# Weight sums of the down projection on GpSimd: made during the up projection instead of during the heads

## The chip, the cores and the metric

The kernel runs on one core of one Trainium2 chip, in one launch. Time is device time in microseconds (us), as the median of several runs. Engines have their short names: PE (TensorE matmul), PEld (TensorE weight load), DVE (VectorE), ACT (ScalarE), POOL (GpSimd), SP (SyncE, whose queue here issues nearly all transfers).

## The reference

One layer of a hybrid decoder for a prompt of 1024 tokens and 8 single tokens (1032 columns): a norm, an input projection, eight HGRN2 heads beside a Mamba-2 mixer, an output projection with residual, and then a gated MLP. The change concerns the MLP's last weight, `w_down`:

```python
h = rmsnorm(x, w['norm2_w'])
gate, val = jnp.split(h @ w['w_up'], 2, axis=-1)
gate, buf_f_new = causal_dwconv(gate, buf_f, w['ffn_conv_w'], w['ffn_conv_b'])
x = x + (jax.nn.silu(gate) * val) @ w['w_down']     # (1032, 2816) @ (2816, 1024)
```

## The kernel before

All matrix products run in fp32 precision as three products of rounded parts (high x high, high x low, low x high). The program is written as one stream of matmuls in a fixed order on PE (`manual_schedule`); the other engines' instructions are placed by a scheduler, in an order that is fixed when the program is built, and each engine works through its own in that order. Work that goes beside the matmuls is handed out by a count of matmul steps: `after(n, work)` (a list that `tick` counts down) and `spread(pieces, n)`, which takes the next piece of a generator every n ticks, one tick for each matmul of the main stream.

The stages on the profile's clock: input projection and scan of the mixer to some 390 us; the heads (390 to 880, the rest of the input projection runs between their matmuls); the output projection with the second norm (to some 1050); the up projection (to about 1500); the down projection.

The MLP's two products use a fast 2x2 block scheme with seven block products, named `p1` to `p7`. For the down projection four of the seven need sums of weight blocks. `down_sums` (L1192) makes them ahead: 22 pieces, for each of 11 row blocks and 2 column halves. A piece fetches 2 x 256 KB of `w_down` to a tile `wq` (L193, in `fetch`), adds on POOL four times 128x256 in place (L1202), and stores 512 KB to `wsum_d` in device memory (L1204). The tile has tag "g" with one buffer, so a piece's fetch comes behind the store of the piece before. The down projection reads `wsum_d` in `dw_load`, first in its unit 0, which is loaded during the last channel tile of the up projection (`last_step`).

In the kernel before, these pieces start with the job "conv" (L1220), after the second head's projection, one step of a piece every 26 ticks, and run during heads 1 to 6.

The up projection (`ups`, L1649) goes over 22 channel tiles `j`. A tile has 14 products, (name, half) for seven names and two halves of the tokens, each 12 matmuls of 258 columns, so 168 ticks in a tile. From the second tile on they come in the order `p1 p6 p5 p7 p2 p4 p3`, both halves of each. What belongs to one tile:

- `up_load` (L1394): two loads of 512 KB of up weights `ws` for the next tile (L1401), each to one of two buffers, on SP.
- `up_sums` (L1410): four sums `wt` of 128x512 on POOL (L1417), of both loads.
- `up_split` (L1427): the rounded parts `wh` on ACT (L1440) and the rests `wl` on DVE (L1441), two names at a time.
- `Up`: evictions. `p1` and `p5` are copied by ACT (`us`, L1463 and L1471), `p6`, `p7`, `p2`, `p4` and `p3` are added by DVE (L1467, L1475, L1483, L1491, L1498). After `p7` POOL makes `val` (L1476) and `us` (L1477) for that half; DVE's eviction of `p3` (L1498) reads this `us`.
- `up_close`: convolution, SiLU and product on ACT and DVE; `act_sets` stores the activation's blocks to `act_d` (L1521, SP), 4 stores for an even tile, and for an odd one 10, both in the tile after.

Products `p1`, `p7`, `p3` go to three psum banks in turn (`ua`), the other four to four banks (`ub`): so `p4` of a half takes the bank that `p5` of the same half left.

Of the kernel before, what the change touches and what calls it, by code (L numbers as in the profile page):

```python
# [51 lines left out]
def hybrid_layer(  # L52
# [30 lines left out]
    def tl(tag, name, dt=F32):  # L83
        w, n = TAGS[tag]
        return (work if tag in ("hT", "big", "e", "g") else tmp).tile([P, w], dt, tag=tag, bufs=n, name=nm(name))
# [104 lines left out]
    def fetch(dst, src):  # L190

        with tc.issue_after(last_w[0].ins):
            SP.dma_start(dst, src)  # L193
# [44 lines left out]
    def job(name, load, run):  # L238
        jobs.append((name, load, run))

    def after(n, work):

        item = [n, work]
        later.append(item)
        return item
# [7 lines left out]
    def tick():  # L253
        for item in list(later):
            item[0] -= 1
            if item[0] <= 0:
                later.remove(item)
                item[1]()

    def spread(pieces, n, then=None):  # L260

        def go():
            if next(pieces, 0) is None:
                after(n, go)
            elif then is not None:
                then()
        go()
# [75 lines left out]
    def conv_state(src2d, nrow, ntile, out):  # L343
        def rows(j0):
            rt = half("rt")
            nj = min(4, ntile - j0)
            fetch(rt[:nrow, :nj * P], src2d[:, j0 * P:(j0 + nj) * P])
            return rt, nj

        nxt = rows(0)  # L350
        for j0 in range(0, ntile, 4):
            yield
            (rt, nj), nxt = nxt, rows(j0 + 4) if j0 + 4 < ntile else None
            ps = bank("cst", "nx")
            for j in range(nj):
                PE.transpose(ps[:, j * nrow:(j + 1) * nrow], rt[:nrow, j * P:(j + 1) * P], ident[:nrow, :nrow])
            V.tensor_copy(out[:, j0:j0 + nj, :], ps[:, :nj * nrow].rearrange("p (j r) -> p j r", r=nrow))
# [407 lines left out]
    def ssm_conv_state():  # L765
        for j0 in range(0, XT, 4):
            yield
            ps = bank("l11", "nx")
            for j in range(4):
                PE.transpose(ps[:11, j * P:(j + 1) * P], last11[:, j0 + j, :], ident)  # L770
            csr = keep.tile([16, 512], F32, tag="csr", bufs=1, name=nm("csr"))
            V.tensor_copy(csr[:11, :512], ps[:11, :])
            cl = slice(j0 * P, (j0 + 4) * P)
            SP.dma_start(cs_prompt[0, 0, :, cl], csr[0:3, :512])
            SP.dma_start(cs_sample[0, :, 2, cl], csr[3:11, :512])
        SP.dma_start(cs_sample[0, :, 0:2, :], state_conv_ssm[0, :, 1:3, :])
# [16 lines left out]
    def once(work):  # L793
        def run():
            work()
            return
            yield
        return run
# [63 lines left out]
    def head_in(h):  # L862
        t = {}

        def f_end():
            f, k = t["f"], tl("big", "k")
            A.activation(f[:, :NT], f[:, :NT], AF.Identity, bias=lbt[:, 0, h:h + 1], scale=lbt[:, 1, h:h + 1])
            V.tensor_scalar(k[:, :NT], f[:, :NT], -1.0, 1.0, op0=ALU.mult, op1=ALU.add)
            t["k"] = k

        for n, off, func in (("f", OFF_F, AF.Sigmoid), ("q", OFF_Q, AF.Silu), ("v", OFF_I, AF.Copy),
                             ("sg", OFF_G, AF.Silu)):
            def evict(c, cs, ps, n=n, func=func):
                t["out"] = A.activation(t[n][:, cs], ps, func)

            def begin(n=n):
                t[n] = tl("e" if h == 0 and n == "f" else "big", n)

            if h == H - 1 and n == "sg":
                in_job_last(f"{n}{h}", off + h * P, evict, begin)  # L880
            else:
                in_job(f"{n}{h}", off + h * P, evict, begin, f_end if n == "f" else None)
        return t
# [308 lines left out]
    def down_sums():  # L1192
        src = w_down[0].rearrange("(i two p) (gv h c) -> h i p two gv c", two=2, p=P, gv=2, h=2)
        for i in range(DK):
            for h in range(2):
                t = tl("g", "wq")[:, :DM]
                for two in range(2):
                    fetch(t[:, two * 512:(two + 1) * 512].rearrange("p (gv c) -> p gv c", gv=2), src[h, i][:, two])
                yield
                g1, v1, g2, v2 = (t[:, n * 256:(n + 1) * 256] for n in range(4))  # L1200
                for out, x_, y_ in ((v2, v1, v2), (v1, g1, v1), (g1, v2, g1), (g2, g1, g2)):
                    G.tensor_tensor(out, x_, y_, op=ALU.add)  # L1202
                yield
                SP.dma_start(wsum_d[h].rearrange("q m p k c -> p k (q m) c")[:, i],  # L1204
                             t.rearrange("p (q c) -> p q c", c=P))
                yield
# [3 lines left out]
    def conv_states():  # L1210
        yield from ssm_conv_state()
        yield from conv_state(state_conv_ffn[0].rearrange("b r d -> (b r) d"), 16, FT, fbufT)
        yield
# [3 lines left out]
    heads[0] = head_in(0)  # L1217
    ssm_gate(1)
    heads[1] = head_in(1)
    job("conv", None, once(lambda: (spread(conv_states(), 60), spread(down_sums(), 26))))  # L1220
    for h in range(2, H):
        heads[h] = head_in(h)

# [425 lines left out]
    def ups(j, seq):  # L1649

        us_ = up_open(j)
        for n, (name, i) in enumerate(seq):
            yield from us_[i].mul(name)
            if n == 2 and j + 1 < FT:
                up_load(j + 1)
            if n == 5 and j == 0:
                up_sums(1)
            if n in (5, 9, 13) and j + 1 < FT:
                up_split(j + 1, (5, 9, 13).index(n))
            if n == 1 and j:  # L1660
                up_split(j, 3)
            if j == FT - 1:
                last_step(n)
        up_close(j, us_[0])

    with tc.manual_schedule(engines={mybir.EngineType.PE}):
# [25 lines left out]
        after(24, lambda: spread(second, 1))  # L1692
        for _ in ups(0, [(name, i) for i in range(2) for name in FIRST]):
            tick()
        for j in range(1, FT):
            for _ in ups(j, [(name, i) for name in ORDER for i in range(2)]):
                tick()
# [134 lines left out]
```

## Time and profile before

| | us |
|---|---|
| median of three timed runs (lowest, highest) | 1748.21 (1746.71, 1750.33) |
| the profiled execution, its own time | 1748.51 |
| its span, first to last instruction | 1746.6 |
| PE busy | 1704.6 (98%) |
| DVE busy | 1180.5 (68%) |
| ACT busy | 838.3 (48%) |
| POOL busy | 485.6 (28%) |
| POOL adds on `wq`, 88 of them, from 433.9 to 786.7 | 83.3 |

In rows of the profile an instruction has its start, its length, engine, line, operation and its tiles as out<-in; in brackets stands how long its engine was idle before it and what ended that. `x4` is four in a row. In lists of waits three numbers stand behind each pair: us in total, how often, and the longest. The table of stretches gives each engine's busy time and, in brackets, its instructions. Busy time of PE is made of pipelined matmuls, so a busy PE is not PE at its peak.

### The profile page before, as it was taken

The numbers are of one execution on the slowest core, as the hardware profiler recorded it, in microseconds if no ns is written. First come the engines' busy times: TensorE is split into PE (matmuls) and PEld (weight loads), VectorE is DVE, ScalarE is ACT, GpSimd is POOL, SyncE is SP. The second block draws the span as 40 slices with busy tenths as digits, with TensorE's granted clock in tenths as the row PEclk, the third lists the DMA queues.
The fourth block names the chain that finished last, engine by engine and source line by source line (L and its number), as shares of the span: only waits on it lengthen the run. The fifth ranks groups of instructions, "written<-read, shape, count | busy, mean of one in ns | idle before, by whom it ended". The sixth has DMA issues, their size and how long they took to land.

```text
span 1746.6 us, 39082 instructions
## 1 busy us (share of the span) xinstructions
PE 1704.6 (98%) x15967; PEld 1650.3 (94%) x15967; DVE 1180.5 (68%) x2053; ACT 838.3 (48%) x1507; POOL 485.6 (28%) x500
## 2 busy tenths in 40 slices
PE   7999999999999999999999998999999999999998
PEld 7999998998999999999899998999999999999998
DVE  4657888467755655664755678867777777775664
ACT  6478688443443444444344444334433334444344
POOL 1102242111433422440102124554445554000001
PEclk9999999999999999999999999999999999999999
DMA  5133574563444443444556442323333323786463
GB/s 158 37 82 93 144 211 139 154 178 120 147 140 127 133 147 111 139 131 124 159 169 204 127 136 58 104 92 95 101 113 113 92 92 96 251 270 229 152 190 123
DMA packets 319689, 239.31 MB, mean 137 GB/s; under 512 B 18380, under 2 KB 287734, under 8 KB 319494
## 3 DMA queue, kind: packets, MB, share of 16 engines
q1 hardware_dynamic: 319222, 236.72, 45.1%
q8 instruction: 125, 2.05, 0.5%
q14 instruction: 54, 0.44, 0.1%
q0 software_dynamic: 288, 0.10, 0.0%
HBM read 178.18 MB, written 58.77 MB: 136 GB/s over the span
## 4 chain that ended last, share of the span: by engine, by line
PE 41%; DVE 4%; DMA 2%; ACT 1%; issue 1%; SPq 1%; DVEq 0%; ACTq 0%
PE ub L94 13%; PE dn L94 11%; PE ua L94 9%; PE mm L94 7%; DMA at<-act_d 1%; DMA ws<-in_w_out_dram 1%; DVE x L1320 1%; DVE wl L1094 0%; PE fin L1761 0%; SPq L193 0%; DVE ul L1331 0%; DMA x<-x_d 0%; DVE wl L1441 0%; DMA act_d<-fext 0%; DVE fcv L370 0%
## 5 line engine op out<-in xcount | busy, mean ns | idle before, releaser
L94 PE MATMUL mm<-hh,wh 128*128 128x344 f32 x1248 | 406.5, 326 | 0.0
L94 PE MATMUL mm<-hl,wh 128*128 128x344 f32 x1248 | 403.9, 324 | 0.0
L94 PE MATMUL mm<-hh,wl 128*128 128x344 f32 x1248 | 402.9, 323 | 0.0
L94 PEld LDWEIGHTS mm<-hh,wh 128*128 128x128 f32 x1248 | 234.9, 188 | 2.9 <-issue 0.9
L94 PEld LDWEIGHTS mm<-hh,wl 128*128 128x128 f32 x1248 | 235.1, 188 | 2.1 <-issue 1.0
L94 PEld LDWEIGHTS mm<-hl,wh 128*128 128x128 f32 x1248 | 234.9, 188 | 2.2 <-issue 0.9
L94 PE MATMUL ub<-uh,wh 128*128 128x258 f32 x704 | 199.4, 283 | 2.1 <-DVE fext L1491 1.6
L94 PE MATMUL ub<-ul,wh 128*128 128x258 f32 x704 | 199.6, 283 | 1.5 <-DVE ul L1352 1.5
L94 PE MATMUL ub<-uh,wl 128*128 128x258 f32 x704 | 198.8, 282 | 0.0
L94 PE MATMUL mm<-mx,wh 128*128 128x258 f32 x1024 | 190.9, 286 | 3.2 <-DVE mx L1110 2.3
L94 PEld LDWEIGHTS mm<-mx,wh 128*128 128x128 f32 x1024 | 158.5, 189 | 5.2 <-DVE mx L1110 2.7
L94 PE MATMUL dn<-at,wh 128*128 128x260 f32 (+1 forms) x896 | 163.1, 282 | 0.0
L94 PE MATMUL ua<-uh,wh 128*128 128x258 f32 x528 | 149.2, 283 | 1.1 <-ACT us L1463 0.6
L94 PE MATMUL ua<-ul,wh 128*128 128x258 f32 x528 | 148.9, 282 | 0.0
L94 PE MATMUL ua<-uh,wl 128*128 128x258 f32 x528 | 148.4, 281 | 0.0
L94 PE MATMUL mm<-mx,wl 128*128 128x258 f32 x512 | 145.4, 284 | 1.7 <-DVE wl L1094 1.7
L94 PEld LDWEIGHTS dn<-at,wh 128*128 128x128 f32 x896 | 137.6, 188 | 0.0
L1202 POOL TENSOR_TENSOR wq<-wq 128x256 f32<-128x256 f32 x88 | 83.3, 947 | 189.0 <-DMA wq<-in_w_down_dram 149.6
L94 PEld LDWEIGHTS ub<-uh,wh 128*128 128x128 f32 x704 | 132.9, 189 | 2.5 <-ACT uh L1330 1.8
L94 PEld LDWEIGHTS ub<-ul,wh 128*128 128x128 f32 x704 | 133.1, 189 | 1.9 <-DVE ul L1352 1.9
L94 PEld LDWEIGHTS ub<-uh,wl 128*128 128x128 f32 x704 | 133.1, 189 | 0.0
L94 PE MATMUL dn<-at,wl 128*128 128x260 f32 (+1 forms) x448 | 126.6, 283 | 2.8 <-DVE wl L1607 2.8
(341 smaller groups left out, 3711.9 us busy)
## 6 DMA issues: line engine op xcount, KB each, us to landing
ws<-in_w_in_dram SPq DMA_DIRECT2D x52, 512.0 KB
ws<-in_w_up_dram SPq DMA_DIRECT2D x44, 512.0 KB
at<-act_d SPq DMA_DIRECT2D x77, 258.0 KB
ws<-in_w_out_dram SPq DMA_DIRECT2D x36, 512.0 KB
wq<-in_w_down_dram SPq DMA_DIRECT2D x44, 256.0 KB
wsum_d<-wq SPq DMA_DIRECT2D x22, 512.0 KB
mx<-mix_d SPq DMA_DIRECT2D x32, 258.0 KB
csb<-cs_d SPq DMA_DIRECT2D x32, 256.0 KB
```

The source lines that it names most:

```text
L94: PE.matmul(out, lhsT, rhs, start=start, stop=stop)
L1202: G.tensor_tensor(out, x_, y_, op=ALU.add)
L1320: V.scalar_tensor_tensor(x_, x_, col("n2", m), rs, op0=ALU.mult, op1=ALU.mult)
```

## The change

The 22 pieces are handed out in the up projection, from the start of its second channel tile, one step every 19 ticks, and no longer from the job "conv". A piece has seven steps instead of three: after the fetch two empty ones, then the first add, the second, the third with the fourth, the store. At 7 x 19 = 133 ticks a piece this makes five pieces in about four tiles of 168 ticks.

```diff
                 yield
+                yield
+                yield
                 g1, v1, g2, v2 = (t[:, n * 256:(n + 1) * 256] for n in range(4))
                 for out, x_, y_ in ((v2, v1, v2), (v1, g1, v1), (g1, v2, g1), (g2, g1, g2)):
                     G.tensor_tensor(out, x_, y_, op=ALU.add)
-                yield
+                    if x_ is not v2:
+                        yield
                 SP.dma_start(wsum_d[h].rearrange("q m p k c -> p k (q m) c")[:, i],
                              t.rearrange("p (q c) -> p q c", c=P))
                 yield
...
-    job("conv", None, once(lambda: (spread(conv_states(), 60), spread(down_sums(), 26))))
+    job("conv", None, once(lambda: spread(conv_states(), 60)))
...
         for _ in ups(0, [(name, i) for i in range(2) for name in FIRST]):
             tick()
+        spread(down_sums(), 19)
         for j in range(1, FT):
```

The number and kinds of instructions stay as they are; the order on PE, DVE and ACT stays the same to the row, and only POOL's and SP's change. (Lines behind the first edit are 3 or 4 higher in the changed kernel: L1401 is L1404 there, L1417 is L1420, L1202 and L1204 are L1204 and L1207.)

SP of the kernel before, in channel tile 4 of the up projection: the last activation stores of tile 2, the two loads of up weights `ws` for tile 5, and the first stores that follow.

```order
L1521 DMA act_d<-fext_13056 128x256
L1521 DMA act_d<-fext_13056 128x260
L1401 DMA ws_13653<-in_w_up_dram 128x8x128
L1401 DMA ws_13655<-in_w_up_dram 128x8x128
L1521 DMA act_d<-val_13326 128x256
```

SP of the changed kernel at the same place:

```order
L1524 DMA act_d<-fext_12891 128x256
L1524 DMA act_d<-fext_12891 128x260
L193 DMA wq_13276<-in_w_down_dram 128x2x256
L1207 DMA wsum_d<-wq_13276 128x8x128
L193 DMA wq_13499<-in_w_down_dram 128x2x256 x2
L1404 DMA ws_13512<-in_w_up_dram 128x8x128
L1207 DMA wsum_d<-wq_13499 128x8x128
L1404 DMA ws_13514<-in_w_up_dram 128x8x128
L193 DMA wq_13698<-in_w_down_dram 128x2x256
L1524 DMA act_d<-val_13170 128x256
```

The end of piece 4 (`wq_13276`), all of piece 5 (`wq_13499`) and the first fetch of piece 6 stand where the two loads of up weights stood alone, and the store of piece 5 stands between the two. The same picture comes again four, eight and twelve tiles later.

POOL of the kernel before, from the end of tile 3's group of sums to tile 4's group (`wt` of `ws_13653` and `ws_13655`):

```order
L1417 TENSOR_TENSOR wt_13392<-wt_13388,ws_13382 128x512
L1502 MEMSET fext_13588 128x2
L1504 COPY fext_13588<-fbufT 128x8x2
L1476 TENSOR_TENSOR val_13326<-us_13422,us_13458 128x258
L1477 TENSOR_TENSOR us_13380<-us_13422,us_13380 128x258
L1476 TENSOR_TENSOR val_13326<-us_13437,us_13475 128x258
L1477 TENSOR_TENSOR us_13407<-us_13437,us_13407 128x258
L1417 TENSOR_TENSOR wt_13657<-ws_13655 128x512
```

POOL of the changed kernel at the same place:

```order
L1420 TENSOR_TENSOR wt_13239<-wt_13235,ws_13229 128x512
L1505 MEMSET fext_13443 128x2
L1507 COPY fext_13443<-fbufT 128x8x2
L1204 TENSOR_TENSOR wq_13276<-wq_13276 128x256 x3
L1479 TENSOR_TENSOR val_13170<-us_13270,us_13309 128x258
L1480 TENSOR_TENSOR us_13227<-us_13270,us_13227 128x258
L1204 TENSOR_TENSOR wq_13276<-wq_13276 128x256
L1479 TENSOR_TENSOR val_13170<-us_13288,us_13326 128x258
L1480 TENSOR_TENSOR us_13255<-us_13288,us_13255 128x258
L1204 TENSOR_TENSOR wq_13499<-wq_13499 128x256 x4
L1420 TENSOR_TENSOR wt_13516<-ws_13514 128x512
```

Piece 4 is split around the first half's `val` and `us`, three adds ahead of them and one behind; piece 5's four adds stand ahead of the next group of sums.

## The prediction

> **What bounds the kernel now.** The page comes first, for the engine that is busy all the time; then the table of stretches, for the stage that the work leaves and the stage that it enters.
>
> ```profile
> PE 1704.6 (98%) x15967; PEld 1650.3 (94%) x15967; DVE 1180.5 (68%) x2053; ACT 838.3 (48%) x1507; POOL 485.6 (28%) x500
> L1202 POOL TENSOR_TENSOR wq<-wq 128x256 f32<-128x256 f32 x88 | 83.3, 947 | 189.0 <-DMA wq<-in_w_down_dram 149.6
> ...
> core 0: us, PE busy (x) PEld busy (x) DVE busy (x) ACT busy (x) POOL busy (x), PEclk, DMA share, GB/s
> 430.00:800.00 370.00, 365.31 (x4787) 347.65 (x4787) 225.77 (x370) 160.46 (x247) 133.51 (x124) 1.00 0.45 133
> 1080.00:1500.00 420.00, 418.88 (x3490) 418.46 (x3489) 313.64 (x551) 168.09 (x303) 199.43 (x206) 1.00 0.34 106
> 1080.00:1100.00 20.00, 19.37 (x162) 19.16 (x161) 17.43 (x28) 9.56 (x17) 11.17 (x9) 1.00 0.27 81
> ```
>
> TensorE is busy in both stages, the heads (430 to 800) and the up projection (1080 to 1500). What the change can win is what TensorE waits for in the heads; what it can lose is a wait that the up projection hardly has today. So the waits of TensorE and of its weight loads are read next, first for 430 to 800, then (last two rows) for 1080 to 1500.
>
> ```profile
> PE a L94 <- DVE q L925: 2.3, 4, 1.2
> PE a L94 <- issue: 1.7, 1, 1.7
> PE cst L356 <- DVE od L699: 0.5, 1, 0.5
> PEld a L94 <- DVE tt L927: 1.1, 5, 0.2
> PEld cst L356 <- DVE od L699: 0.8, 1, 0.8
> PEld cst L356 <- DVE sg L1054: 0.2, 1, 0.2
> ...
> PE ua L94 <- ACT us L1463: 0.6, 1, 0.6
> PE ua L94 <- DVE val L1498: 0.5, 1, 0.5
> ```
>
> The 88 adds run on POOL, which no wait of TensorE names. They touch TensorE only through VectorE: 2.3 us of waits for `q` (L925) and 0.5 for the reciprocal root (L699); with the weight loads' waits for VectorE (1.1, 0.8, 0.2) that is 4.9 us. In the up projection TensorE waits 1.1 us in 420.
>
> **The change part by part.** *Leaving the heads.* The 83.3 us of adds and the 66 transfers go from a place where nobody waits for them. The gain is at most the 4.9 us above and at least nothing, since some of those waits are for VectorE's own chain. I take 2.3, the four waits for `q`, the row that names a VectorE step which shares its time with the adds.
>
> *Entering the up projection: room on POOL.* 88 adds of 947 ns are 83 us more on POOL's 199.43 of 420: 67%, so POOL does not become the bound on average. What counts is the order on POOL and on SP. One channel tile of the up projection lasts 20.2 us (1240.87 to 1261.03 in the first fence below, two successive weight loads). In it POOL makes four weight sums `wt`, then `val` and `us` for each half, and is free for some 10 us before the next weights land.
>
> ```profile
> 1240.87 4.81 SPq L1401 DMA_DIRECT2D ws<-in_w_up_dram  x2
> 1261.03 4.80 SPq L1401 DMA_DIRECT2D ws<-in_w_up_dram  x2
> ...
> 1249.07 1.46 POOL L1417 TENSOR_TENSOR wt<-ws 128x512 f32<-128x512 f32 x1 [9.63 <-DMA ws<-in_w_up_dram]
> ...
> 1254.79 0.11 POOL L1502 MEMSET fext<- 128x2 f32 x1
> ...
> 1255.42 1.19 POOL L1476 TENSOR_TENSOR val<-us,us 128x258 f32<-128x258 f32 x1
> 1256.58 0.74 POOL L1477 TENSOR_TENSOR us<-us,us 128x258 f32<-128x258 f32 x1
> ...
> 1269.41 1.43 POOL L1417 TENSOR_TENSOR wt<-ws 128x512 f32<-128x512 f32 x1 [10.67 <-DVE fext L1548]
> ```
>
> In the changed order most pieces stand either in that free time or, three adds and one, around the first `val` and `us`. The exception is where two pieces follow each other without a `wt` group between them: pieces 4 and 5, 9 and 10, 14 and 15, 19 and 20, in channel tiles 4, 8, 12 and 16. SP then has: store of the first piece, two fetches of the second, the first half of the next up weights, the store of the second piece, and only then the second half of the up weights. SP is one queue: the fetch reuses the only `wq` buffer and waits for the store to land, the second store waits for POOL, and the up weights `ws` are queued behind it. How long each link takes stands in the heads, where the same transfers run: store to next fetch, fetch to POOL's start, and four adds.
>
> ```profile
> 547.12 0.37 SPq L1204 DMA_DIRECT2D wsum_d<-wq  x1
> ...
> 550.52 1.20 SPq L193 DMA_DIRECT2D wq<-in_w_down_dram  x2
> 555.58 3.82 POOL L1202 TENSOR_TENSOR wq<-wq 128x256 f32<-128x256 f32 x4 [8.49 <-DMA wq<-in_w_down_dram]
> ...
> 603.15 1.20 SPq L193 DMA_DIRECT2D wq<-in_w_down_dram  x2
> 607.40 3.50 POOL L1202 TENSOR_TENSOR wq<-wq 128x256 f32<-128x256 f32 x4 [7.69 <-DMA wq<-in_w_down_dram]
> ...
> 629.01 1.21 SPq L193 DMA_DIRECT2D wq<-in_w_down_dram  x2
> 635.47 3.18 POOL L1202 TENSOR_TENSOR wq<-wq 128x256 f32<-128x256 f32 x4 [11.71 <-DMA wq<-in_w_down_dram]
> 781.55 5.16 POOL L1202 TENSOR_TENSOR wq<-wq 128x256 f32<-128x256 f32 x4
> ```
>
> Put on the tile quoted above, whose `wt` group began at 1249.07: POOL is through `wt`, memset and copy at 1255.4. Three adds of the first piece (3 x 0.947 = 2.8) end at 1258.3; `val` and `us` (1.19 + 0.74) at 1260.2; the fourth add at 1261.1. The store goes out and the fetch follows 3.4 us later (547.12 to 550.52): 1264.5. POOL has the data 4.9 us after that (5.06 and 4.25 in two of the rows, 6.46 in the third; I take the middle of the denser end): 1269.4. Four adds, 3.8: 1273.2. Issuing the store and then the second up load, 0.4 each: 1274.0. The load lands 3.5 us later (1265.83, the end of the pair issued at 1261.03, to POOL's 1269.41 is 3.6; 1245.68 to 1249.07 is 3.4): the `wt` group starts at 1277.5 instead of 1269.41.
>
> Who waits for it? ACT's order is unchanged, and in it the copy that empties a psum bank (`us`, L1471) stands behind the cast of the second `wt` sum:
>
> ```profile
> 1272.57 0.62 ACT L1440 CAST wh<-wt 128x512 fp32r<-128x512 f32 x1 [2.41 <-POOL wt L1417]
> 1273.09 0.37 ACT L1471 COPY us<-ub 128x258 f32<-128x258 f32 x1
> ...
> 1278.44 0.42 DVE L1491 TENSOR_TENSOR fext<-us,ub 128x258 f32<-128x258 f32 x1 [0.57 <-PE ub L94]
> ```
>
> That copy empties the second product of `p5`; the bank is the one of four that the second product of `p4` takes, six products on, and TensorE begins that when the first product of `p4` is done (1278.44, where VectorE takes it). Today the copy ends at 1273.46, 5.0 us early. So a `wt` group later than 1269.4 + 5.0 = 1274.4 stops TensorE, and 1277.5 stops it for 3.1 us. Four times: 12.4 us.
>
> The bounds of one such place: with adds of 0.74 (635.47: 3.18 for four), a wait of 4.25 and a landing of 3.4, the chain ends at 1274.9, a stall of 0.5, which is nothing within these steps. With adds of 1.29 (781.55), 6.46 and a landing of 5.5 (below) it ends near 1284.4, a stall of 10. So 0 to 40 us for the four; I stay at the mean duration of the group (947 ns), since VectorE is busier here (313.64 of 420) than in the heads (225.77 of 370).
>
> ```profile
> 1200.56 4.81 SPq L1401 DMA_DIRECT2D ws<-in_w_up_dram  x2
> 1210.89 1.29 POOL L1417 TENSOR_TENSOR wt<-ws 128x512 f32<-128x512 f32 x1 [11.98 <-DMA ws<-in_w_up_dram]
> ```
>
> These rows are also a trial that the kernel made itself: that `wt` group came 2 us later in its tile than usual, and TensorE did not wait (its list of waits for 1140 to 1500 is empty). The slack is real, and 8 us are more than it.
>
> *After such a place.* The next piece's adds stand ahead of the following `wt` group, their store ahead of both halves of the up weights, so the next tile is late too, by 3 to 5 us, about its slack; and the piece after that sits between `wt` and `val`, where `us` feeds VectorE's eviction of `p3` (L1498). I put 1 us on each of the four (0 to 3): 4 us.
>
> *The first pieces.* The first piece stands on POOL ahead of `val` of tile 0, its buffer comes free when the second half's norm is done, and VectorE is nearly full there (17.43 of 20). I put 1 us, 0 to 3.
>
> *Stores and fetches.* 66 transfers of 256 and 512 KB move into a stage with a DMA share of 0.34, below the 0.45 that they leave; the sums are first read at the start of the down projection, and the last piece is stored about 3 tiles before. Cost nothing; if that cover were gone, each late load would stop the first units.
>
> *VectorE.* An add on POOL lengthens a VectorE step with two operands from memory:
>
> ```profile
> 1260.27 0.69 DVE L1441 TENSOR_TENSOR wl<-ws,wh 128x512 fp32r<-128x512 f32 x1
> ...
> 1261.48 0.42 DVE L1498 TENSOR_TENSOR val<-us,ua 128x258 f32<-128x258 f32 x1
> ...
> 1214.24 1.11 DVE L1441 TENSOR_TENSOR wl<-wt,wh 128x512 fp32r<-128x512 f32 x1 [5.16 <-ACT wh L1440]
> ...
> 1213.51 1.29 POOL L1417 TENSOR_TENSOR wt<-ws,ws 128x512 f32<-128x512 f32 x1
> 1214.77 1.74 POOL L1417 TENSOR_TENSOR wt<-wt,ws 128x512 f32<-128x512 f32 x1
> ```
>
> From 0.69 to 1.11 us beside POOL: 0.42 x 88 = 37 us more on VectorE's 313.64, 83% of the stage, hidden behind TensorE. [...]
>
> The sum against the profiled execution (1748.51 us, span 1746.6; the median of the three timed runs is 1748.21, 0.3 below): -2.3 + 12.4 + 4 + 1 = +15.1, so 1763.6 us.
>
> **The rivals.** *Absorbed.* If wait, adds and landing all sit at their short ends, the four places cost nothing, and the change is worth -2.3 + 1 = -1.3: 1747.2 us. For it speaks the chain's low end, 0.5 us past the slack; against it the mean rows, all in one direction. It decides at 3.1 us less in the chain.
>
> *Faster.* The heads give back all that VectorE owes TensorE there, 4.9 us, and the up projection hides everything: 1743.6 us. The mechanism is VectorE's scan steps without POOL beside them; it needs the second up load out before 1270.9 on the clock of the quoted tile. Against it: only 2.3 of the 4.9 are a wait of TensorE for a step of the scan.
>
> *Late `us` as well.* In the eight tiles in which a piece is split around `val` and `us`, three adds delay `us`, and VectorE, which takes the products in order, stands at L1498. By mean rows `us` ends at 1260.2, where L1498 of the same tile ran at 1261.48 (among the VectorE rows above), so it is hidden; with adds of 1.29 each and a `wt` group 3 us late it is not, and some 2 us are lost eight times: 1763.6 + 16 = 1780 us. [...]
>
> *No effect on TensorE at either place*, since the moved work is on engines that it does not name: 1748.5 us; this lies inside the absorbed case and is counted with it.
>
> **How the numbers follow.** A measurement of this kernel can tell about 0.2%, 3.5 us, from no change. Forecast 0.60, absorbed 0.20, faster 0.13, late `us` 0.07. Faster by over 0.2% is the third case: 0.13. Within 0.2%: the absorbed case and a sliver of the forecast with stalls under 1 us, 0.21. Slower: 0.66. The forecast's own range is 1753 to 1777 (the four stalls at 0.5 to 6.5 us each, the rest as taken). The range that should hold 8 times in 10 reaches from the absorbed case to the late `us`: 1745 to 1780.
>
> **What would show it.** Right: TensorE waits `ub <- ACT us` in the up projection, four times, 2 to 6 us each, about 80 us apart; SP's second `ws` issued some 10 us after the first; PE busy in 1080 to 1500 down by some 15 us. In the heads the waits for L925 shrink. Wrong: no such wait although the order is as told, the `wt` group after a double piece starting under 5 us late; or stalls in every tile; or a heads stage shorter by clearly more than 4.9 us, which would mean that adds on POOL cost TensorE time that its waits do not show.

## The result, and the profile after

The changed kernel takes 1812.31 us (median of six runs, 1806.82 to 1816.66), the kernel before 1749.22 beside it (six runs, 1745.08 to 1752.65): a ratio of 1.0363, 95% interval 1.0339 to 1.0387. The forecast was 1763.6 with a range up to 1780. The direction was right, the size was not: some 63 us are lost where 15 were foreseen.

The head of the page of the changed kernel:

```profile
span 1808.8 us, 39041 instructions
...
PE 1725.0 (95%) x15967; PEld 1667.6 (92%) x15967; DVE 1177.1 (65%) x2053; ACT 835.9 (46%) x1507; POOL 509.7 (28%) x500
```

Its table of stretches, heads and up projection:

```profile
430.00:800.00 370.00, 369.49 (x4832) 351.50 (x4831) 207.96 (x373) 162.40 (x250) 50.06 (x36) 1.00 0.25 72
1080.00:1500.00 420.00, 372.72 (x2945) 368.38 (x2944) 277.70 (x455) 134.55 (x247) 272.29 (x258) 0.95 0.47 137
```

The span is 62.2 us longer. TensorE's idle time grows from 42.0 (1746.6 - 1704.6) to 83.8, by 41.8; the same 15967 matmuls are busy 20.4 longer, and the granted clock of the up projection is 0.95. The heads are better, 369.49 us of work in 370 in place of 365.31: 4.2 us. No engine is full in the up projection: POOL works 272 of 420 us, VectorE 278.

TensorE's waits from 1080 to 1500, all that the list has:

```profile
PE ub L94 <- ACT us L1474: 28.7, 10, 6.7
PE ua L94 <- DVE val L1501: 18.5, 9, 2.1
```

Both waits that the prediction spoke of are there, the second as well, though it stood as a rival with 0.07. Here is one double place on the clock, rows of SP, POOL, ACT and PE:

```profile
1228.42 1.29 POOL L1420 TENSOR_TENSOR wt<-ws 128x512 f32<-128x512 f32 x1 [7.79 <-DMA ws<-in_w_up_dram]
...
1240.38 0.38 SPq L1207 DMA_DIRECT2D wsum_d<-wq  x1
1243.59 1.21 SPq L193 DMA_DIRECT2D wq<-in_w_down_dram  x2
1244.90 0.55 SPq L1404 DMA_DIRECT2D ws<-in_w_up_dram  x1
...
1252.16 0.37 SPq L1207 DMA_DIRECT2D wsum_d<-wq  x1
1252.62 0.53 SPq L1404 DMA_DIRECT2D ws<-in_w_up_dram  x1
...
1257.97 1.26 POOL L1420 TENSOR_TENSOR wt<-ws 128x512 f32<-128x512 f32 x1 [5.83 <-DMA ws<-in_w_up_dram]
...
1261.13 0.37 ACT L1474 COPY us<-ub 128x258 f32<-128x258 f32 x1
...
1261.55 0.58 PE L94 MATMUL ub<-uh,wh 128*128 128x258 f32 x1 [6.66 <-ACT us L1474]
```

The chain is the forecast one, link by link: `wt` to the store 11.96 us, store to fetch 3.2, and so on to the next `wt`; 29.55 in all, where the prediction's links add up to 28.4 (1249.07 to 1277.5). The missing 1.1 is in the last link, from the issue of the second `ws` to `wt`: 5.35 us (1252.62 to 1257.97), where 0.4 and 3.5 were taken. But TensorE waits 6.66 us, not 3.1. Why, the tiles around it show, by the starts of their `wt` groups. The first and the last row bound the 16 tiles of the four cycles:

```profile
1106.37 1.35 POOL L1420 TENSOR_TENSOR wt<-ws 128x512 f32<-128x512 f32 x1 [4.62 <-DVE fext L1551]
...
1204.61 1.29 POOL L1420 TENSOR_TENSOR wt<-ws 128x512 f32<-128x512 f32 x1 [6.66 <-DMA ws<-in_w_up_dram]
...
1280.92 1.28 POOL L1420 TENSOR_TENSOR wt<-ws 128x512 f32<-128x512 f32 x1 [7.36 <-DMA ws<-in_w_up_dram]
...
1301.54 1.43 POOL L1420 TENSOR_TENSOR wt<-ws 128x512 f32<-128x512 f32 x1 [6.27 <-DVE fext L1551]
...
1494.58 1.53 POOL L1420 TENSOR_TENSOR wt<-ws 128x512 f32<-128x512 f32 x1 [6.17 <-DMA ws<-in_w_up_dram]
```

One cycle of four tiles lasts 23.81, 29.55, 22.95 and 20.62 us (1204.61 to 1228.42, 1257.97, 1280.92, 1301.54) in place of 20.16 each. The double tile costs 9.4, but its two neighbours, which hold a single piece each, cost 3.7 and 2.8; the fourth tile costs 0.5. Over the 16 tiles between the first and the last row it is 388.2 / 16 = 24.3 each, 4.1 us too long; 16 x 4.1 = 66 less the 4.2 of the heads is the 62. So the loss is in three tiles of every four, and TensorE meets a double place with its 5.0 us of slack already used: in the tile before, it waits 0.3 us for the same copy (its waits from 1230 to 1250, beside 2.1 for `val`).

### The profile page after: what moved, and what is told of

Same layout as the page of the kernel before. It is cut to its first block, busy times and chain, and to the rows that moved or that the text cites. A ratio compares the mean times of both kernels' runs of the same rounds, so it can differ in the third digit from the quotient of the medians.

```text
span 1808.8 us, 39041 instructions
## 1 busy us (share of the span) xinstructions
PE 1725.0 (95%) x15967; PEld 1667.6 (92%) x15967; DVE 1177.1 (65%) x2053; ACT 835.9 (46%) x1507; POOL 509.7 (28%) x500
## 4 chain that ended last, share of the span: by engine, by line
PE 25%; POOL 9%; issue 8%; DVE 4%; DMA 4%; ACT 1%; SPq 1%; DVEq 0%; POOLq 0%; ACTq 0%
PE dn L94 10%; PE mm L94 7%; PE ub L94 4%; POOL wq L1204 4%; PE ua L94 3%; POOL wt L1420 3%; POOL us L1480 1%; DMA wq<-in_w_down_dram 1%; DMA wsum_d<-wq 1%; POOL val L1479 1%; SPq L193 1%; DMA ws<-in_w_out_dram 1%; DMA at<-act_d 1%; DVE x L1323 1%; DMA ws<-in_w_up_dram 0%
## 5 line engine op out<-in xcount | busy, mean ns | idle before, releaser
L94 PE MATMUL mm<-hh,wh 128*128 128x344 f32 x1248 | 406.5, 326 | 0.0
L94 PE MATMUL mm<-hl,wh 128*128 128x344 f32 x1248 | 403.8, 324 | 0.0
L94 PE MATMUL mm<-hh,wl 128*128 128x344 f32 x1248 | 402.5, 323 | 0.0
L94 PEld LDWEIGHTS mm<-hh,wh 128*128 128x128 f32 x1248 | 234.9, 188 | 2.9 <-issue 0.9
L94 PEld LDWEIGHTS mm<-hl,wh 128*128 128x128 f32 x1248 | 234.9, 188 | 2.3 <-issue 0.9
L94 PEld LDWEIGHTS mm<-hh,wl 128*128 128x128 f32 x1248 | 234.9, 188 | 2.0 <-issue 1.0
L94 PE MATMUL ub<-uh,wh 128*128 128x258 f32 x704 | 205.0, 291 | 31.6 <-ACT us L1474 31.0
L94 PE MATMUL ub<-ul,wh 128*128 128x258 f32 x704 | 203.5, 289 | 0.7 <-DVE ul L1355 0.7
L94 PE MATMUL ub<-uh,wl 128*128 128x258 f32 x704 | 202.4, 288 | 0.0
L94 PE MATMUL mm<-mx,wh 128*128 128x258 f32 x1024 | 190.7, 286 | 2.9 <-DVE mx L1110 2.2
L94 PE MATMUL ua<-uh,wh 128*128 128x258 f32 x528 | 154.3, 292 | 19.0 <-DVE val L1501 18.5
L94 PEld LDWEIGHTS ub<-uh,wh 128*128 128x128 f32 x704 | 137.1, 195 | 34.4 <-ACT us L1474 33.7
L94 PE MATMUL dn<-at,wh 128*128 128x260 f32 (+1 forms) x896 | 164.0, 283 | 0.0
L94 PEld LDWEIGHTS mm<-mx,wh 128*128 128x128 f32 x1024 | 158.6, 189 | 4.5 <-DVE mx L1110 2.6
L94 PE MATMUL ua<-ul,wh 128*128 128x258 f32 x528 | 152.7, 289 | 0.0
L94 PE MATMUL ua<-uh,wl 128*128 128x258 f32 x528 | 152.1, 288 | 0.0
L94 PE MATMUL mm<-mx,wl 128*128 128x258 f32 x512 | 145.4, 284 | 1.6 <-DVE wl L1094 1.5
L1444 DVE TENSOR_TENSOR wl<-wt,wh 128x512 fp32r<-128x512 f32 x88 | 90.8, 1051 | 84.5 <-ACT wh L1443 84.5
L94 PEld LDWEIGHTS ub<-ul,wh 128*128 128x128 f32 x704 | 137.4, 195 | 1.2 <-DVE ul L1355 1.2
L94 PEld LDWEIGHTS dn<-at,wh 128*128 128x128 f32 x896 | 138.4, 189 | 0.0
L94 PEld LDWEIGHTS ub<-uh,wl 128*128 128x128 f32 x704 | 137.2, 195 | 0.0
L1050 POOL TENSOR_TENSOR sg<-sg,sq 128x512 f32<-128x512 f32 x16 | 24.4, 1542 | 375.8 <-DVE sq L701 231.1
```

What stands on the lines that cost most here:

```text
L94: PE.matmul(out, lhsT, rhs, start=start, stop=stop)
L1050: G.tensor_tensor(oh, oh, sq[hf], op=ALU.mult)
L1444: V.tensor_tensor(lo[:, cs], sums[name], hi[:, cs].bitcast(F32), op=ALU.subtract)
```

## The experiments

First the question was which of three things makes the waits: theory Q, SP's queue; rival P, POOL's time; rival D, the bytes. When none of the three alone came out, theory A (the double places) was set against theory B (a loop). Each ratio is to the kernel before, run beside it.

**Stores from POOL's queue.**

```diff
-                SP.dma_start(wsum_d[h]...
+                G.dma_start(wsum_d[h]...
```

> The 22 stores of the sums go out from POOL's queue, right behind their own adds, and no longer from SP's. Theory Q (the queue: on SP the second load of up weights stands behind a store that waits for POOL's adds): at the four double places the second `ws` goes out 7 us earlier, the four stalls (22.2 us of waits `ub <- ACT us`) and the half-clock work behind them go, some 35 to 40 us; the waits of 2.1 us for `val` stay in part: 1765 to 1780 us. Rival P (POOL's time: adds ahead of `wt`, `val` and `us`, drawn out beside VectorE): stalls stay, 1800 to 1812 us. Rival D (the bytes of the transfers slow the up weights): 1805 to 1812 us.

Measured 1784.88 us, ratio 1.0213 (1.0200 to 1.0227): some 26 us back, between Q and P. SP's queue matters, but it wasn't free yet: the next piece's fetch, which waits for the adds and the store's landing, still stands ahead of `ws` (below, three fetches take 14.51 us, and both `ws` go out behind them). Rows of SP at the double place, then TensorE's waits from 1080 to 1500:

```profile
1224.99 14.51 SPq L193 DMA_DIRECT2D wq<-in_w_down_dram  x3
1239.54 1.24 SPq L1404 DMA_DIRECT2D ws<-in_w_up_dram  x2
```

```profile
PE ua L94 <- DVE val L1501: 16.5, 7, 4.8
PE ub L94 <- ACT us L1474: 13.5, 5, 4.1
```

**No adds.**

```diff
-                    G.tensor_tensor(out, x_, y_, op=ALU.add)
```

> The changed kernel without its 88 adds (so the sums of the down projection are left out): fetches and stores stay where they are. Theory Q: the store at a double place still waits for its fetch to land, so the second `ws` still goes out late, by some 5 us in place of 10, which is about the slack: stalls of 0 to 2 us, 1748 to 1760 us. Rival P: all stalls go, 1744 to 1748 us. Rival D: they stay, 1790 to 1812 us.

Measured 1741.26 us, ratio 0.9964 (0.9951 to 0.9977), better than either theory said. All transfers are in the up projection, still on SP, and TensorE does not wait there at all:

```profile
1080.00:1500.00 420.00, 420.00 (x3504) 420.00 (x3503) 311.23 (x550) 167.98 (x300) 197.74 (x204) 1.00 0.53 159
```

Rival D falls. Between Q and P the run does not decide, since without the adds both the store's wait for POOL and POOL's own time are gone. It does show that a store that waits only for its fetch costs TensorE nothing here.

**Small transfers.**

```diff
+                n = 256 if i == h == 0 else 8
-                    fetch(t..., src[h, i][:, two])
+                    fetch(t...[:, :, :n], src[h, i][:, two][:, :, :n])
...
-                SP.dma_start(wsum_d[h]...
+                SP.dma_start(small_d[h, i], t...[:, :, 248:256])
```

> All 88 adds and 66 issues stay in the up projection, but each transfer moves 8 columns in place of 256 (so the sums are left out; the full transfers run in the heads without adds, to fill their place in memory). At the double places the order on SP is the same but for the store, which stands ahead of both `ws`. Theory Q: the chain store, fetch, adds, store is shorter by the landing of the bytes, some 3 of 10 us, and keeps its adds: the four stalls shrink to 2 to 3 us each and the half-clock work mostly goes, 1765 to 1785 us. Rival P: 1800 to 1812 us. Rival D: no stall, 1746 to 1752 us.

Measured 1790.92 us, ratio 1.0240 (1.0224 to 1.0257). That is in none of the three ranges. Two thirds of the loss stay with hardly a byte moved in the up projection. The third that went is in the waits for `us`; it is not the bytes' alone, since the store of a double place stands elsewhere in SP's order too. The waits for `val` are no fewer than in the changed kernel:

```profile
PE ua L94 <- DVE val L1518: 21.5, 11, 2.8
PE ub L94 <- ACT us L1491: 9.5, 7, 4.0
```

**The heads without the adds.**

```diff
-                for out, x_, y_ in ((v2, v1, v2), (v1, g1, v1), (g1, v2, g1), (g2, g1, g2)):
-                    G.tensor_tensor(out, x_, y_, op=ALU.add)
```

> The kernel before without its 88 adds (so the sums of the down projection are left out): what the heads can win by the move. By the step of the prediction: 2.3 us less, bounds 0 and 4.9, so a ratio of 0.9987 (0.9972 to 1.0). If adds on POOL cost TensorE time that its waits do not show, clearly more than 4.9 us.

Measured 1743.04 us, ratio 0.9977 (0.9963 to 0.9991), so 4.0 us (1.6 to 6.5). With the 4.2 us of the table of stretches this is near the upper end of the step's bounds. What came back, this kernel's lists of waits for 430 to 800 show, first TensorE's whole list, then the weight loads' waits for VectorE:

```profile
PE cst L356 <- DVE od L699: 0.5, 1, 0.5
PEld a L94 <- DVE tt L927: 1.3, 6, 0.2
PEld cst L356 <- DVE od L699: 0.8, 1, 0.8
PEld cst L356 <- DVE sg L1054: 0.2, 1, 0.2
```

Of the kernel before's list the waits for `q` (2.3) and the one row `issue` (1.7) are gone, 4.0 us together; the other waits for VectorE are still there, and in the changed kernel the lists are the same.

**One piece in each tile.** Nowhere are two pieces in a row.

```diff
-    job("conv", None, once(lambda: (spread(conv_states(), 60), spread(down_sums(), 26))))
+    job("conv", None, once(lambda: (spread(conv_states(), 60), spread(islice(sums, 6), 26))))
...
+        after(44, lambda: spread(sums, 56))
         for j in range(1, FT):
```

> Pieces 1 and 2 stay in the heads, the other 20 run in the up projection in the three steps of the kernel before, one every 168 ticks, so one in each channel tile and nowhere two in a row: no double place is left. On POOL nine of them are still split three and one around the first `val`, and on SP every store stands ahead of both `ws`. Theory A (the prediction's: double places make the loss): 1744 to 1752 us. Theory B (any adds ahead of `val` and `us`, and any store on SP ahead of `ws` that waits for adds): 9 waits of 2 to 3 us for `val` and tiles with late `ws`, 20 to 45 us with the half-clock work behind them: 1765 to 1790 us.

Measured 1786.76 us, ratio 1.0220 (1.0206 to 1.0235). Theory A, which was the prediction's, falls: without a double place 38 us are still lost, in waits of at most 2.5 us:

```profile
PE ua L94 <- DVE val L1500: 19.6, 11, 2.1
PE ub L94 <- ACT us L1473: 9.7, 6, 2.5
```

**Adds behind `us`, stores from POOL's queue.**

```diff
-                    G.tensor_tensor(out, x_, y_, op=ALU.add)
+                    with tc.issue_after((pin[0] or summed[0] or last_w[0]).ins):
+                        G.tensor_tensor(out, x_, y_, op=ALU.add)
...
-                SP.dma_start(wsum_d[h]...
+                G.dma_start(wsum_d[h]...
...
-            G.tensor_tensor(self.u2, self.f, self.u2, op=ALU.subtract)
+            pin[0] = G.tensor_tensor(self.u2, self.f, self.u2, op=ALU.subtract)
```

> As one piece per tile, with two edits: the four adds are pinned behind the second half's `us` on POOL, where it is free for some 10 us, and the stores go out from POOL's queue, so that no `ws` stands behind one. The same adds and transfers in the same stage. Theory B: no wait is left in the up projection, and what is left is the heads' gain less two pieces, 1742 to 1747 us. Rival P (the amount of POOL's work and its contention with VectorE, wherever it stands): 1765 us or more.

Measured 1747.18 us, ratio 0.9987 (0.9975 to 0.9999), 0.2 us above theory B's range. Rival P falls as a matter of amount: the stage now has more of POOL than in the changed kernel (332 us in place of 272) and longer adds (1266 ns in place of 1106), and TensorE waits 1.1 us in it. Its row of the stretches, and the group of the adds in the same stretch:

```profile
1080.00:1500.00 420.00, 418.87 (x3488) 418.40 (x3487) 335.23 (x543) 165.21 (x299) 332.08 (x304) 1.00 0.52 157
```

```profile
L1205 POOL TENSOR_TENSOR wq<-wq 128x256 f32<-128x256 f32 x80 | 101.3, 1266 | 4.9 <-issue 0.2
```

POOL is at 79%, VectorE at 80%, an add takes 1266 ns (947 in the heads of the kernel before), and nearly all of that is hidden. VectorE stands 26.8 us in the stage at the eviction of `p3` until POOL's `us` is there (25 times), and TensorE hardly feels it.

**The same pins, stores on SP.** The only edit against the kernel above is `SP` for `G` in the store.

> The same pins, but the stores on SP again, each ahead of both `ws`. Theory B: a loop from tile to tile, `ws` landing 8.2 + group and `fext` 6.5 + `val` and `us` 3.4 + four adds 3.8 to 5.3, some 22 to 23 us against a tile of 20.2, less what of the landing is not waited for: a stall of 0 to 2.5 us in each of 19 tiles, 1745 to 1790 us; the waits are for `us` of ACT and for `val`. Theory A: no stall, 1744 to 1750 us.

Measured 1811.83 us, ratio 1.0359 (1.0346 to 1.0373): one queue for another makes 65 us, as much as the whole change, without a double place and without an add ahead of `val`. The expected range ended too low: 63 us over 19 tiles are 3.3 a tile, where at most 2.5 were expected. One turn of the loop, rows of POOL and SP:

```profile
1273.31 1.28 POOL L1422 TENSOR_TENSOR wt<-ws 128x512 f32<-128x512 f32 x1 [7.38 <-DMA ws<-in_w_up_dram]
...
1283.16 5.73 POOL L1205 TENSOR_TENSOR wq<-wq 128x256 f32<-128x256 f32 x4
...
1288.92 0.38 SPq L1207 DMA_DIRECT2D wsum_d<-wq  x1
1289.39 1.94 SPq L1406 DMA_DIRECT2D ws<-in_w_up_dram  x2
...
1296.23 1.29 POOL L1422 TENSOR_TENSOR wt<-ws 128x512 f32<-128x512 f32 x1 [7.34 <-DMA ws<-in_w_up_dram]
```

`wt`, `fext`, `val` and `us` 9.85, adds 5.73, store and issue 0.5, landing of `ws` 6.84: 22.92 us against 20.16, and then it begins again. Every link waits for the one before. This turn is the shortest of the stage; the mean of 19, from the `wt` group at 1084.24 to the one at 1532.12, is 23.6 us. In the kernel before, `ws` waits for no result of POOL's last step, so there is no such loop; its POOL idles some 10 us in each tile, and that idle time looked like room.

**The loop with two of four adds.**

```diff
-                for out, x_, y_ in ((v2, v1, v2), (v1, g1, v1), (g1, v2, g1), (g2, g1, g2)):
+                for out, x_, y_ in ((v2, v1, v2), (v1, g1, v1)):
```

> As fixed behind with the stores on SP, but with two of the four adds of each piece (so half of the sums are left out); every queue keeps its order and every transfer stays. Theory B (a loop from tile to tile, adds, store, `ws`, `wt`, `val` and `us`, adds, of 22.9 us by the rows of that kernel, in place of the tile's 20.2): two adds of 1.43 us less make the loop 20.1 us, TensorE hardly waits, 1744 to 1755 us. If the stores or the wait for POOL cost by themselves, whatever the length of the loop, or if the loss went with the amount of adds (half of it): 1775 us or more.

Measured 1753.96 us, ratio 1.0025 (1.0011 to 1.0040). Half the adds bring back 58 of 63 us, not half of the loss, as a loop does that comes down to the tile's own length. What is left of it from 1080 to 1500:

```profile
PE ua L94 <- DVE val L1503: 4.9, 8, 1.2
PE ub L94 <- ACT us L1476: 0.5, 1, 0.5
```

**The store behind both `ws`.** SP for everything, adds pinned as above.

```diff
-                SP.dma_start(wsum_d[h]...
-                yield
+                if pin[0]:
+                    yield
+                with tc.issue_after(last_w[0].ins):
+                    SP.dma_start(wsum_d[h]...
```

> All four adds, pinned behind the second half's `us`, all transfers on SP, and the store pinned behind both `ws` of the tile in place of ahead of them. Theory B: the loop is open, since no up weight waits for the adds: 1742 to 1750 us, as with the stores on POOL's queue. If SP as the queue of the stores mattered in itself, or the bytes beside `ws`: 1765 us or more.

Measured 1746.14 us, ratio 0.9984 (0.9970 to 0.9997). Not the queue but the place in it decides. Rows of SP:

```profile
1254.99 5.51 SPq L1410 DMA_DIRECT2D ws<-in_w_up_dram  x2
1260.67 0.46 SPq L1210 DMA_DIRECT2D wsum_d<-wq  x1
```

**Adds ahead of `val`.** As the kernel with the adds behind `us` and the stores from POOL's queue, but the pin is the last `wt` add in place of `us`, and the pieces are handed out from tick 158 of the tile in place of 44.

```diff
-                G.tensor_tensor(sums[name], x_, y_, op=ALU.add)
+                add.last = G.tensor_tensor(sums[name], x_, y_, op=ALU.add)
...
         add("p4", p6, g2)
+        pin[0] = add.last
...
-        after(44, lambda: spread(sums, 56))
+        after(158, lambda: spread(sums, 56))
```

> As fixed behind, stores from POOL's queue, but the four adds pinned behind the `wt` group, which is ahead of `val` and `us` of both halves. No `ws` stands behind a store. Theory B: `us` some 4 to 5 us later in every tile, VectorE stands at the eviction of `p3`, and TensorE waits 1 to 3 us for `val` in most of the 20 tiles: 1765 to 1800 us. If only the queue of SP counted: 1742 to 1748 us.

Measured 1795.61 us, ratio 1.0272 (1.0257 to 1.0287). The range of theory B held: 47 us are lost, and nearly all of TensorE's waits are of the second kind:

```profile
PE ua L94 <- DVE val L1504: 27.9, 15, 3.5
```

That the place on POOL does this alone is not shown, though. No `ws` stands behind a store on SP, but the next piece's two fetches wait for the store to land (249.0 us in the stage, 18 times), and here they stand right ahead of both `ws`:

```profile
1275.84 1.20 SPq L193 DMA_DIRECT2D wq<-in_w_down_dram  x2
1277.14 2.25 SPq L1406 DMA_DIRECT2D ws<-in_w_up_dram  x2
```

The second `ws` then waits once more, 1.6 us on average, for VectorE's `wl` of its old buffer, which comes behind the late evictions of `p3`; and all 19 `wt` groups wait for `ws`. So this kernel has a loop from tile to tile as well, 22.4 us in the turn from 1261.68 to 1284.09, that goes through POOL, VectorE and SP. How much of it SP's queue makes was not separated by a run.

## Why the prediction was wrong, point by point

- *Leaving the heads*, -2.3: 4.2 by the table, 4.0 by the run without adds. Too small, inside its bounds of 0 to 4.9, but not by the rival "faster", in which all 4.9 us of waits for VectorE come back. Only the 2.3 for `q` did; 2.8 us of the others are still there. The rest is the row `a L94 <- issue: 1.7`, which the prediction shows and puts at nothing without a reason. It goes with the adds, not with the transfers, which stay in the heads without adds; what that wait was for, the profile does not show.
- *The double places*, four stalls of 3.1: they are there, `ub <- ACT us`, of 4.9, 6.7, 6.5 and 4.1 us (the largest in the windows 1145 to 1165, 1250 to 1275, 1340 to 1360 and 1440 to 1470), 22.2 in place of 12.4. The chain of links was sized right to 1.1 us in 28.4. The step that failed is "5.0 us of slack": it was read from a kernel in which every tile starts rested, and set against each late `wt` as if the lateness ended there. In the changed kernel nothing of it was left at the double place shown above. (The lower bound of a place is added up wrongly as well: four adds of 3.18 us are 0.795 each, not 0.74, so the chain ends at 1275.5 and the stall is 1.1 us, not 0.5; the upper end adds up to 1283.8, not 1284.4.)
- *After such a place*, 1 us on each: this is the term that was mis-sized most. The other waits of 1080 to 1500 sum to 25.0 (28.7 + 18.5 - 22.2). Of these, 18.5 are the waits for `val` (next but one point) and 6.5 more of those for `us`. For the tile behind a double place the prediction saw that the store stands ahead of both `ws`, but let the slack pay for it once more; the tile is 2.8 us longer. For the single piece ahead of a double place, which stands "in that free time", it did not ask what is queued behind the store; that tile is 3.7 us longer. In one piece per tile there are no double places, and 38 us stay.
- *The slack's own trial*, a `wt` group 2 us late without a wait: right, but it was a single delay. Where a tile is 2.8 us too long again and again, slack is used once.
- *Late `us`*: given 0.07 and 2 us eight times; it came nine times, up to 2.1, 18.5 us in all, so its size was right and its chance too small. By mean rows `us` was to end 1.3 us ahead of L1498 (1260.2 and 1261.48), room that a late `wt` group uses up: VectorE stood at that eviction for POOL's `us` 17 times, 21.8 us in all, and once in the kernel before. With the adds ahead of `val` in every tile it is nearly the only wait, but SP's queue has a part there too.
- *Stores and fetches* at nothing, *VectorE* hidden: both right, as no adds and adds behind `us` show. DMA's share of 0.47 to 0.53 and VectorE's 80% cost nothing in themselves. VectorE's work in the stage grew by 21.6 us beside 80 adds (335.23 less 313.64); the row's 0.42 us an add would make 34.
- *The first piece*, +1: no cost shows. The waits of TensorE around it, from 1050 to 1085 us, sum to 4.0 us in place of 4.2 in the kernel before; one of 2.3 for `us` at about 1066 stands beside smaller ones.
- *The clock* was no term at all, and PE's busy time grew by 20.4. Its part is not simply a cost to be added: where the loop sets the pace, TensorE would have waited in that time. The kernel with the pins and stores on SP loses the same 63 us at a mean clock of 0.994 over the span (0.985 here, 0.998 before). How much the clock adds in the tiles that no loop paces was not separated by a run.

"What would show it" named a sign of failure: "stalls in every tile". It came in three tiles of every four.

## What to carry to other kernels

When a moved step ends in a transfer on a shared queue, list what stands behind that transfer, and follow it until the chain reaches the moved step again: if it does, add up the whole turn and set it against the period of the work, because slack pays for one late start and not for one in every period. Idle time of an engine (POOL's 10 us in each tile) is room only if the work put in it starts after the due results and nothing due is queued behind its end. The second condition is shown here by one edit: the same 80 adds in the same place on POOL cost 63 us or gain 2, by the place of one store in SP's queue. The first is shown only together with SP's queue. The version with the store behind both `ws` beats the kernel before by 0.16% (0.03 to 0.30), and some 4 us were to be had at most.

## What the runs showed of the hardware

The granted clock fell to half (0.50) in the two stalls below, and came back to 1.00 only some 5.5 and 3.5 us after TensorE had work again. Stretches of the changed kernel, around the 6.66 us stall and then around a wait of 2.12 us, whose row stands below them:

```profile
1256.00:1258.00 2.00, 0.00 (x0) 0.00 (x0) 0.00 (x0) 0.00 (x0) 0.03 (x1) 0.72 0.85 238
...
1262.00:1264.00 2.00, 2.00 (x11) 2.00 (x11) 2.00 (x5) 0.96 (x2) 2.00 (x2) 0.50 0.61 173
1264.00:1266.00 2.00, 2.00 (x11) 2.00 (x10) 2.00 (x5) 1.14 (x2) 2.00 (x5) 0.50 0.14 46
1266.00:1268.00 2.00, 2.00 (x15) 2.00 (x14) 2.00 (x6) 1.26 (x1) 2.00 (x3) 0.72 0.00 0
1268.00:1270.00 2.00, 2.00 (x20) 2.00 (x19) 2.00 (x3) 0.62 (x1) 1.92 (x2) 1.00 0.00 0
...
1192.00:1194.00 2.00, 1.26 (x11) 1.05 (x9) 1.59 (x2) 1.90 (x3) 2.00 (x2) 1.00 0.01 4
1194.00:1196.00 2.00, 0.62 (x3) 0.62 (x4) 1.10 (x2) 0.00 (x0) 2.00 (x4) 0.86 0.00 0
1196.00:1198.00 2.00, 2.00 (x11) 2.00 (x11) 0.67 (x2) 0.00 (x0) 1.95 (x2) 0.50 0.75 207
1198.00:1200.00 2.00, 2.00 (x15) 2.00 (x14) 2.00 (x3) 0.29 (x1) 0.00 (x0) 0.78 1.04 290
```

```profile
1195.38 0.53 PE L94 MATMUL ua<-uh,wh 128*128 128x258 f32 x1 [2.12 <-DVE val L1501]
```

After the long stall eleven matmul records touch a stretch of 2 us at 0.50, where twenty do at 1.00 (1268 to 1270). Full clock came some 5.5 us after work began again at 1261.55, and some 3.5 us after 1195.38. In the long stall the 0.72 from 1256 to 1258, taken as a mean of 1.00 and 0.50, puts the fall at about 1256.9, 2.0 us after TensorE went idle (1261.55 - 6.66 = 1254.89). The wait of 2.12 us was followed by 0.50 too. Not every such wait does it: one of 2.56 us in the kernel with stores from POOL's queue left the clock at 1.00, and what makes the difference is not shown here (the wait, and the stretch that holds its end):

```profile
1342.82 0.39 PE L94 MATMUL ub<-uh,wh 128*128 128x258 f32 x1 [2.56 <-ACT us L1474]
1342.00:1344.00 2.00, 1.18 (x9) 1.18 (x10) 1.47 (x3) 1.67 (x4) 2.00 (x2) 1.00 0.17 50
```
